# A rebuilt opening of a two-layer diffusion block: tokens first, and shift and scale from float32 products on raw adaLN weights

## The chip, the core and the metric

The kernel runs on one core of one Trainium2 chip. TensorE multiplies (in the rows PE is its products and PEld its weight loads), VectorE (DVE), ScalarE (ACT) and GpSimd (POOL) do the elementwise work, and SyncE (SP) issues the transfers from HBM. The metric is the device time of one execution in microseconds, the median of several runs; less is better.

## The reference

Two layers work on 256 latent tokens and 256 context tokens of width 1024. Ahead of each sublayer every token is normalized, scaled and shifted; shift, scale and gate come from a conditioning vector (`c` for the latent tokens, `c_ctx` for the context tokens) through one wide matrix per layer. Only the first sublayer's start matters here:

```python
def _rms(x, eps=EPS):
    return x * lax.rsqrt(jnp.mean(x * x, axis=-1, keepdims=True) + eps)

def _modulate(x, shift, scale):
    return _rms(x) * (1 + scale) + shift

def _ada_params(cond, w, b):                 # w: (1024, 6144)
    m = jnp.dot(jax.nn.silu(cond), w) + b
    return jnp.split(m[..., None, :], 6, axis=-1)   # sh1, sc1, g1, sh2, sc2, g2

def _chunk_gmlp(h, w_in, norm_g, w_s, b_s, w_out):
    u, v = jnp.split(jax.nn.gelu(h @ w_in), 2, axis=-1)   # v: 2048 columns
    ...

# layer 0, the same for the context tokens with c_ctx
sh1, sc1, g1, sh2, sc2, g2 = _ada_params(c, ada_w[0], ada_b[0])
m_lat = _chunk_gmlp(_modulate(h, sh1, sc1), ...)
```

The rest of layer 0, its FFN, the attention layer and the second FFN are the same before and after the change.

## The kernel before

**Layout.** Activations are kept transposed: `hT[k]` holds channels k\*128 to k\*128+127 (k = 0 to 7) on the partitions and all 512 tokens in the free dimension. A product that needs float32 accuracy is made of three fp32r products: each operand is split into a high part (`xhi`, `whi`, a rounded copy that ACT writes) and a low part (`xlo`, `wlo`, the difference, on DVE), and `mm3` (lines 61 to 63) adds hi·hi, hi·lo and lo·hi.

**Weight stream.** `Stream` (`ws`) brings the weights of all large products in the order of use. `load` issues 512 KB per half of a piece into `raw` (four buffers), `split` makes `whi` and `wlo` from a half, `get` hands a piece to TensorE, and `release` splits the pieces that may come next (two buffers of `whi` and `wlo`).

**The opening** (lines 304 to 467, pool `start`) makes the modulated tokens for the first sublayer and the first quarter of v. It runs over u = 0 to 7; step u makes shift and scale of channel chunk u:

- `a_load(u)`: two transfers of 512 KB, the columns of `ada_w[0]` for scale (w = 1) and shift (w = 0) of chunk u, in `araw`.
- `a_split(u)`: `ahi` by ACT (line 320) and `alo` by POOL for the scale and DVE for the shift (line 322).
- `ada_mm(u)`: sixteen products (lines 327 and 328) whose stationary operand `cvr` has four columns (high and low part of the two conditioning vectors) and whose moving operand is 256 columns of `ahi` or `alo`. The result has 4 partitions; ACT copies it out (`ada_sb`, line 344), two transposes bring it back onto 128 partitions (`ps_adaT`, line 350), and two DVE additions make `mods` (lines 355 and 356).
- `x_modulate(u)`: `modt` (DVE, line 378), `xhi` (ACT, line 382) and `xlo` (DVE, line 384) for both token groups.
- `v_first(u - 2)`: the twelve products of chunk u - 2 with the first 512 columns of v, four token tiles by three parts.

Ahead of that, the four token tiles `xt` (512 KB each) are squared and summed by ACT (line 430), transposed on TensorE (`x_trans`, line 366) and copied to `hT`; `r` is the reciprocal root per token, and `rb` its broadcast through TensorE (`ps_rb`, lines 444 and 448). In the opening the order on ACT, DVE and TensorE is near that of the code (`manual_schedule`); elsewhere a scheduler places the instructions.

**After the opening**, v has three more quarters (96 products each), interleaved with `bg(1)`: background units that accumulate the rest of the adaLN vector on DVE (`ada_acc`, lines 295 and 297) from `ada_raw`, two buffers of 512 KB (line 246), and fold and transpose it in `bg_stage` (lines 256 to 264). Then u, the position mixing (`ps_mix`, line 579) and the rest follow.

Of the kernel before, what the change touches and what calls it, by code (L numbers as in the profile page):

```python
# [11 lines left out]
F32 = mybir.dt.float32  # L12
F32R = mybir.dt.float32r
# [22 lines left out]
def dit_kernel(ctx: ExitStack, tc: tile.TileContext, x, c, cx, c_ctx, ada_w, ada_b, gm_w_in, gm_norm_g,  # L36
# [13 lines left out]
    def f(ap):  # L50
        return ap.bitcast(F32)
# [13 lines left out]
    class Stream:  # L65
# [22 lines left out]
        def split(self, upto, eng=None):  # L88

            while self.ns < min(upto, 2 * len(self.specs)):  # L90
                i, half = self.ns // 2, self.ns % 2
                _, _, kc, _, cols = self.specs[i]
                n = kc * cols
                if half == 0:
                    self.tiles[i] = [wp.tile([P, 2048], F32R, tag=t, name=t, bufs=self.HB)[:, :n] for t in ("whi", "wlo")]
                hi, lo = self.tiles[i]
# [117 lines left out]
        return mods[l][:, which * 8 + kc, cond:cond + 1]  # L214

    cs = cp.tile([P, 2, KC], F32, name="cs")
    cvr = cp.tile([P, KC, 4], F32R, name="cvr")
# [84 lines left out]


    with tc.tile_pool(name="start", bufs=1) as st:
        araw, ahl = {}, {}

        def a_load(u):
            for w in (1, 0):
                t = st.tile([P, KC, P], F32, tag="araw", name="araw", bufs=4)
# [21 lines left out]
        a_load(0)  # L331
        xts = []
        for t in range(4):
            xt = st.tile([P, D], F32, name=f"xt{t}")
            sp.dma_start(xt, (x if t < 2 else cx)[0, (t % 2) * P:(t % 2 + 1) * P, :])
            xts.append(xt)
            if t == 1:
                dma_vecs(1)
        a_load(1)
        ws.load(1)  # L340

        def ada_out(ps, u):
            sb = kp.tile([4, 256], F32, tag="ada_sb", name="ada_sb")
            act.copy(sb, ps[:4, :])
            return sb

        def ada_mods(sb, u):
            pt = aux("ps_adaT")
            for w in range(2):
                pe.transpose(out=pt[:, w * 4:w * 4 + 4], in_=sb[:, w * P:(w + 1) * P], identity=ident[:4, :4])  # L350
            p3 = pt[:, :8].rearrange("p (w c) -> p w c", w=2)
            m = mods[0][:, 0:16, :].rearrange("p (w k) c -> p w k c", w=2)[:, :, u, :]
            ab = adab[:, 0, 0:16].rearrange("p (w k) -> p w k", w=2)[:, :, u:u + 1].broadcast_to([P, 2, 2])
            tmp = kp.tile([P, 2, 2], F32, tag="ada_t", name="ada_t")
            dve.tensor_tensor(tmp, p3[:, :, 0:2], ab, op=ALU.add)
            dve.tensor_tensor(m, tmp, p3[:, :, 2:4], op=ALU.add)

        rb = st.tile([P, T], F32, name="rb")

        xps = {}  # L360

        def x_trans(k, eng):

            ps = acc("ps_xT")
            for t in range(4):
                pe.transpose(out=ps[:, t * P:(t + 1) * P], in_=xts[t][:, k * P:(k + 1) * P], identity=ident)
            xps[k] = ps
            if eng:
                eng(hT[k], ps)

        def x_modulate(k, part=None):

            if part in (None, 0):
                xm[k] = []
                for s in range(2):
                    sl = slice(s * S, (s + 1) * S)
                    t = kp.tile([P, S], F32, tag="modt", name="modt")
                    dve.scalar_tensor_tensor(t, hT[k][:, sl], mod(0, 1, k, s), rb[:, sl], op0=ALU.mult, op1=ALU.mult)
                    xm[k].append((sl, t))
            for s, (sl, t) in enumerate(xm[k]):  # L380
                if part in (None, 1):
                    act.activation(xhi[k][:, sl], t, AF.Identity, bias=mod(0, 0, k, s))
                if part in (None, 2):
                    dve.scalar_tensor_tensor(xlo[k][:, sl], t, mod(0, 0, k, s), f(xhi[k][:, sl]),  # L384
                                             op0=ALU.add, op1=ALU.subtract)

        xm = {}

        def ada_step(u):
            ps = aux("ps_ada", 256)  # L390
            ada_mm(ps, u)
            sb = ada_out(ps, u)
            if u < KC - 1:
                a_split(u + 1)
            if u < KC - 2:
                a_load(u + 2)
            if u < 4:
                ws.split(u + 1)
            if u >= 2:
                v_first(u - 2)  # L400
            ada_mods(sb, u)
            x_modulate(u)

        pss, wv = [], []

        def v_first(k):
# [5 lines left out]
            for t in range(4):  # L412
                mm3(pss[t], xr(k, t * P, (t + 1) * P), (w[0][:, k % 4, :], w[1][:, k % 4, :]),
                    start=k == 0, stop=k == KC - 1)
            if k == 3:
                ws.release()

        with tc.manual_schedule(engines={mybir.EngineType.Activation, mybir.EngineType.DVE, mybir.EngineType.PE}):

            load_vecs(0)  # L420
            act.activation(cs, vecs[:, 0:16].rearrange("p (c k) -> p c k", c=2), AF.Silu)
            act.preload_act_table_set("natural_log_exp_and_others")
            csk = cs.rearrange("p c k -> p k c")
            dve.tensor_copy(cvr[:, :, 0:2], csk)
            dve.tensor_tensor(cvr[:, :, 2:4], csk, f(cvr[:, :, 0:2]), op=ALU.subtract)
            a_split(0)
# [4 lines left out]
            ps_ada = aux("ps_ada", 256)  # L431
            ada_mm(ps_ada, 0)
            load_vecs(1)
            for l in range(2):
                for w in (1, 4):
                    dve.tensor_scalar(adab[:, l, w * 8:w * 8 + 8], adab[:, l, w * 8:w * 8 + 8], 1.0, None, op0=ALU.add)
            x_trans(0, dve.tensor_copy)
            x_trans(1, None)
            x_trans(2, None)
            r = rsqrt(msum, 1.0 / D, 4, "r0")  # L440
            dve.tensor_copy(hT[1], xps[1])
# [4 lines left out]
            sb = ada_out(ps_ada, 0)  # L446
            ada_mods(sb, 0)
            dve.tensor_copy(rb, psr)
            a_split(1, lo=False)
            act.copy(hT[2], xps[2])  # L450
            x_modulate(0, 0)
            a_split(1, hi=False)
            ws.split(1, pool)
            x_modulate(0, 1)
            x_modulate(0, 2)
            for k in range(3, 8):
                x_trans(k, dve.tensor_copy if k in (3, 5, 7) else act.copy)
        a_load(2)
        for u in range(1, KC):
            ada_step(u)  # L460
        for i in range(2, 4):
            dma_vecs(i)
        v_first(KC - 2)
        v_first(KC - 1)
        ws.ahead = True
        ws.release()
        bg_load(2)
# [667 lines left out]
```

## Time and profile before

| what | us |
|---|---|
| median of 3 runs | 1110.42 (1109.51 to 1113.75) |
| the profiled execution | 1113.34 |
| its span on the chip | 1111.6 |
| PE, DVE, ACT, POOL busy in it | 1059.5, 905.6, 547.0, 161.4 |

The span is the stretch from the first to the last instruction; the 1.7 us by which the profiled execution is longer lie around it. Busy time says that an engine had an instruction in work, not that it was at its best. What bounds a stage is read from the stage itself.

### The profile page before, as it was taken

How to read it: one execution, taken by the hardware profiler on the slowest of the kernel's cores; microseconds unless marked ns; L12 is line 12 of the kernel's file. 1: busy time of each engine (PE TensorE's matmuls, PEld its weight loads, DVE VectorE, ACT ScalarE, POOL GpSimd, SP SyncE). 2: the span in 40 equal slices, each digit the busy share in tenths (PEclk: the TensorE clock that was granted, in tenths of full speed). 3: DMA queues.
4: the chain of work that ended last, by engine and by line, in shares of the span. 5: the costliest groups of instructions: out<-in, count | busy, mean ns of one | idle time of the engine just before them, and what ended most of it. 6: DMA issues, size and time to landing. Idle time of an engine off the chain costs nothing.

```text
span 1111.6 us, 15428 instructions
## 1 busy us (share of the span) xinstructions
PE 1059.5 (95%) x5724; PEld 907.3 (82%) x5724; DVE 905.6 (81%) x1518; ACT 547.0 (49%) x921; POOL 161.4 (15%) x131
## 2 busy tenths in 40 slices
PE   4899989999998999999999999989999989999996
PEld 3677868888888888888878888989989878888885
DVE  5978779898999789868686576699988978969696
ACT  6644433323245645224432345456666557757474
POOL 3401101102022011100010002332243040000001
PEclk8999989999999999999999999999999989999998
DMA  8865455544543344676366332333222253565652
GB/s 267 266 210 175 152 171 151 171 138 152 166 146 120 92 147 148 206 225 205 99 205 212 105 118 63 114 106 96 70 84 82 71 171 118 188 200 183 185 176 89
DMA packets 139849, 167.84 MB, mean 151 GB/s; under 512 B 5917, under 2 KB 103934, under 8 KB 139774
## 3 DMA queue, kind: packets, MB, share of 16 engines
q1 hardware_dynamic: 139774, 166.86, 48.1%
q8 instruction: 45, 0.74, 0.3%
q14 instruction: 30, 0.25, 0.1%
HBM read 165.79 MB, written 1.05 MB: 150 GB/s over the span
## 4 chain that ended last, share of the span: by engine, by line
PE 73%; DVE 16%; DMA 4%; issue 3%; ACT 3%; POOL 0%; SPq 0%; DVEq 0%; ACTq 0%; POOLq 0%
PE ps_up L965 7%; PE ps_up L61 6%; PE ps_up L62 6%; PE ps_up L63 6%; PE ps_dn L62 5%; PE ps_dn L63 5%; PE ps_dn L61 5%; DMA ada_raw<-in_ada_w_dram 4%; PE ps_up L967 4%; DVE wlo L101 3%; DVE ada_acc L297 3%; PE ps_u L61 2%; PE ps_u L62 2%; PE ps_u L63 2%; PE ps_wo L62 2%
## 5 line engine op out<-in xcount | busy, mean ns | idle before, releaser
L100 ACT CAST whi<-raw 128x1024 fp32r<-128x1024 f32 (+2 forms) x218 | 218.7, 1023 | 199.9 <-PE ps_dn L62 49.0
L101 DVE TENSOR_TENSOR wlo<-raw,whi 128x1024 fp32r<-128x1024 f32 (+2 forms) x213 | 261.7, 1243 | 51.4 <-ACT whi L100 51.1
L297 DVE SCALAR_TENSOR_TENSOR ada_acc<-ada_raw,cs,ada_acc 128x512 f32<-128x512 f32 x224 | 168.7, 777 | 41.7 <-DMA ada_raw<-in_ada_w_dram 39.7
L63 PE MATMUL ps_up<-xhi,wlo 128*128 128x512 f32 (+1 forms) x384 | 142.4, 372 | 1.0 <-DVE wlo L101 1.0
L61 PE MATMUL ps_up<-xhi,whi 128*128 128x512 f32 (+1 forms) x384 | 143.3, 374 | 0.0
L62 PE MATMUL ps_up<-xlo,whi 128*128 128x512 f32 (+1 forms) x384 | 142.4, 372 | 0.0
L258 POOL TENSOR_TENSOR ada_acc<-ada_acc,ada_half 64x512 f32<-64x512 f32 x16 | 23.4, 1459 | 536.4 <-ACT ada_half L256 397.9
L965 PE MATMUL ps_up<-xhi,whi 128*128 128x512 f32 x352 | 89.7, 397 | 2.5 <-DVE xhi L232 2.5
L63 PEld LDWEIGHTS ps_up<-xhi,wlo 128*128 128x128 f32 x384 | 72.1, 188 | 13.7 <-DVE wlo L101 1.2
L61 PEld LDWEIGHTS ps_up<-xhi,whi 128*128 128x128 f32 x384 | 72.3, 188 | 12.5 <-ACT xhi L231 0.2
L62 PEld LDWEIGHTS ps_up<-xlo,whi 128*128 128x128 f32 x384 | 72.2, 188 | 12.4
L965 PEld LDWEIGHTS ps_up<-xhi,whi 128*128 128x128 f32 x352 | 64.4, 192 | 14.6 <-DVE xhi L232 2.7
L62 PE MATMUL ps_dn<-flo,whi 128*128 128x512 f32 (+1 forms) x200 | 73.0, 365 | 0.7 <-DVE flo L662 0.6
L61 PE MATMUL ps_dn<-fhi,whi 128*128 128x512 f32 (+1 forms) x200 | 73.3, 366 | 0.0
L63 PE MATMUL ps_dn<-fhi,wlo 128*128 128x512 f32 (+1 forms) x200 | 72.7, 364 | 0.0
L61 PE MATMUL ps_wo<-ghi,whi 128*128 128x512 f32 (+1 forms) x160 | 56.1, 354 | 0.1
L62 PE MATMUL ps_wo<-glo,whi 128*128 128x512 f32 (+1 forms) x160 | 55.8, 350 | 0.1
L63 PE MATMUL ps_wo<-ghi,wlo 128*128 128x512 f32 (+1 forms) x160 | 55.7, 349 | 0.0
L61 PE MATMUL ps_u<-xhi,whi 128*128 128x512 f32 x128 | 51.3, 401 | 0.0
L61 PE MATMUL ps_v<-whi,xhi 128*128 128x512 f32 x128 | 51.0, 398 | 0.0
L63 PE MATMUL ps_v<-whi,xlo 128*128 128x512 f32 x128 | 50.2, 393 | 0.6 <-DVE xlo L384 0.6
L967 PEld LDWEIGHTS ps_up<-xhi,wlo 128*128 128x128 f32 x352 | 48.0, 190 | 3.4
(246 smaller groups left out, 2522.5 us busy)
## 6 DMA issues: line engine op xcount, KB each, us to landing
raw<-in_ffn_w_up_dram SPq DMA_DIRECT2D x88, 512.0 KB, 4.2
ada_raw<-in_ada_w_dram SPq DMA_DIRECT2D x80, 512.0 KB, 4.3
raw<-in_ffn_w_down_dram SPq DMA_DIRECT2D x36, 512.0 KB, 3.6
raw<-in_gm_w_in_dram SPq DMA_DIRECT2D x32, 512.0 KB, 4.5
raw<-in_da_w_qkv_dram SPq DMA_DIRECT2D x24, 512.0 KB, 3.7
araw<-in_ada_w_dram SPq DMA_DIRECT2D x16, 512.0 KB, 5.3
raw<-in_gm_w_out_dram SPq DMA_DIRECT2D x16, 512.0 KB, 4.2
raw<-in_ffn_w_down_dram SPq DMA_DIRECT2D x8, 384.0 KB, 3.0
```

Source lines behind the costliest of these rows:

```text
L61: pe.matmul(ps, lhsT=l[0], rhs=r[0], start=start, stop=False)
L62: pe.matmul(ps, lhsT=l[0], rhs=r[1], start=False, stop=False)
L63: pe.matmul(ps, lhsT=l[1], rhs=r[0], start=False, stop=stop)
L100: act.copy(hi[:, sl], raw)
L101: (eng or dve).tensor_tensor(lo[:, sl], raw, f(hi[:, sl]), op=ALU.subtract)
L258: pool.tensor_tensor(a[0][LO, :], a[0][LO, :], t[LO, :], op=ALU.add)
L297: dve.scalar_tensor_tensor(a, raw[:, k, :], cs[:, cd, kc:kc + 1], a, op0=ALU.mult, op1=ALU.add)
L965: pe.matmul(ps, lhsT=wcol(w, k, j)[0], rhs=xhi[k], start=k == 0, stop=False)
L967: pe.matmul(ps[:, :S], lhsT=wcol(w, k, j)[1], rhs=xhi[k][:, :S], start=False, stop=k == KC - 1)
```

## The change: a new order of transfers, and another form of the first products

The token tiles are loaded ahead of the adaLN columns, and `araw` has ten buffers in place of four. `a_split`, `ada_mm`, `ada_out`, `cvr` and the transposes of line 350 go. In their place `ada_mms(u)` multiplies in plain float32: the stationary operand is 128 x 128 of the raw adaLN weights, the moving operand is `csk`, the two conditioning columns. Sixteen products give shift and scale on 128 partitions at once, and `ada_mods` adds the bias in one DVE instruction. `woven(a, b)` emits the products of `b` evenly between those of `a`. POOL has no work in the opening any more. The core of the diff:

```diff
-        def a_split(u, hi=True, lo=True):
-            if hi:
-                ahl[u] = tuple(st.tile([P, KC, 2, P], F32R, tag=t, name=t, bufs=2) for t in ("ahi", "alo"))
-            for w in (1, 0):
-                h, l = (a[:, :, w, :] for a in ahl[u])
-                if hi:
-                    act.copy(h, araw[u, w])
-                if lo:
-                    (pool if w else dve).tensor_tensor(l, araw[u, w], f(h), op=ALU.subtract)
-
-        def ada_mm(ps, u):
-            hi, lo = ahl.pop(u)
-            for kc in range(KC):
-                pe.matmul(ps[:4, :], lhsT=cvr[:, kc, :], rhs=hi[:, kc, :, :], start=kc == 0, stop=False)
-                pe.matmul(ps[:4, :], lhsT=cvr[:, kc, :], rhs=lo[:, kc, :, :], start=False, stop=kc == KC - 1)
+        def ada_mms(u):
+            ps = ada_ps[u] = aux("ps_ada4", 4)
+            def one(w, kc):
+                pe.matmul(ps[:, w * 2:w * 2 + 2], lhsT=araw[u, w][:, kc, :], rhs=csk[:, kc, :],
+                          start=kc == 0, stop=kc == KC - 1)
+            return [lambda w=w, kc=kc: one(w, kc) for w in (1, 0) for kc in range(KC)]
+
+        def ada_mods(u):
+            m = mods[0][:, 0:16, :].rearrange("p (w k) c -> p w k c", w=2)[:, :, u, :]
+            ab = adab[:, 0, 0:16].rearrange("p (w k) -> p w k", w=2)[:, :, u:u + 1].broadcast_to([P, 2, 2])
+            dve.tensor_tensor(m, ada_ps.pop(u).rearrange("p (w c) -> p w c", w=2), ab, op=ALU.add)
+
+        def woven(a, b):
+            n = 0
+            for i, fn in enumerate(a):
+                fn()
+                while n * len(a) < (i + 1) * len(b):
+                    b[n]()
+                    n += 1
...
+            early = [x_trans(k, acc) for k in range(4)]
             for t in range(4):
+                for fns in early:
+                    fns[t]()
                 junk = st.tile([P, D], F32, tag="junk", name="junk")
                 act.activation(junk, xts[t], AF.Square, accum_out=msum[:, t:t + 1])
...
+            woven(ada_mms(0), x_trans(4, acc) + x_trans(5, aux))
+            act.copy(hT[2], xps[2])
+            ada_mods(0)
+            ws.split(1)
+            x_modulate(0)
+            act.copy(hT[3], xps[3])
+            woven(ada_mms(1), x_trans(6, aux) + x_trans(7, acc))
...
+            for u in range(2, KC + 2):
+                if u + 3 < KC:
+                    a_load(u + 3)
+                if u % 2 and u < 8:
+                    ws.load(u // 2 + 2 if u < 7 else 6)
+                if u < KC:
+                    woven(v_mms(u - 2), ada_mms(u))
+                    ada_mods(u)
+                    if u % 2 == 0:
+                        ws.split(u // 2 + 1)
+                    x_modulate(u)
+                else:
+                    woven(v_mms(u - 2), [])
+                if u == 8:
+                    ws.release()
```

TensorE's queue before, where step 2 ends its adaLN products and the products of chunks 0 and 1 with v follow (`ps_ada` is the result on 4 partitions, `ps_v` the v accumulators, the numbers at the names are buffers):

```order
L328 MATMUL ps_ada<-alo,cvr 4x256
L61 MATMUL ps_v<-whi,xhi_96 128x512
L62 MATMUL ps_v<-wlo,xhi_96 128x512
L63 MATMUL ps_v<-whi,xlo_104 128x512
L61 MATMUL ps_v<-whi,xhi_97 128x512
L62 MATMUL ps_v<-wlo,xhi_97 128x512
L63 MATMUL ps_v<-whi,xlo_105 128x512
L61 MATMUL ps_v<-whi,xhi_97 128x512
L62 MATMUL ps_v<-wlo,xhi_97 128x512
L350 MATMUL ps_adaT<-ident,ada_sb 128x4 x2
L327 MATMUL ps_ada<-ahi,cvr 4x256
```

TensorE's queue of the change at the start of step 2, the first products with v:

```order
L388 MATMUL ps_v<-whi,xhi_95 128x512
L320 MATMUL ps_ada_309<-csk,araw 128x2 x2
L388 MATMUL ps_v<-wlo,xhi_95 128x512
L320 MATMUL ps_ada_309<-csk,araw 128x2
L388 MATMUL ps_v<-whi,xlo_103 128x512
L320 MATMUL ps_ada_309<-csk,araw 128x2
L388 MATMUL ps_v<-whi,xhi_95 128x512
```

Sixteen small products with 2 moving columns now stand between the twelve large ones of a step, one or two at a time, where sixteen products of 256 moving columns stood as a block.

The head of SyncE's queue before:

```order
L190 DMA rows_118<-in_c_ctx_dram 8x128
L311 DMA araw<-in_ada_w_dram 128x8x128 x2
L335 DMA xt_125<-in_x_dram 128x1024
L335 DMA xt_127<-in_x_dram 128x1024
L190 DMA rows_129<-in_ada_b_dram 96x128
L335 DMA xt_131<-in_ctx_dram 128x1024
L335 DMA xt_133<-in_ctx_dram 128x1024
L311 DMA araw<-in_ada_w_dram 128x8x128 x2
L83 DMA raw<-in_gm_w_in_dram 128x2x512
L311 DMA araw<-in_ada_w_dram 128x8x128 x3
```

The same place in the change:

```order
L190 DMA rows_117<-in_c_ctx_dram 8x128
L342 DMA xt_120<-in_x_dram 128x1024
L342 DMA xt_122<-in_x_dram 128x1024
L190 DMA rows_124<-in_ada_b_dram 96x128
L342 DMA xt_126<-in_ctx_dram 128x1024
L342 DMA xt_128<-in_ctx_dram 128x1024
L310 DMA araw<-in_ada_w_dram 128x8x128 x4
L83 DMA raw<-in_gm_w_in_dram 128x2x512
L310 DMA araw<-in_ada_w_dram 128x8x128 x4
L83 DMA raw<-in_gm_w_in_dram 128x2x512
L310 DMA araw<-in_ada_w_dram 128x8x128 x6
```

The first adaLN columns move behind the four token tiles, and more of them stand in a row.

## Rows read from the trace of the kernel before

**Rows 1.** Windows: busy us per engine (instructions), TensorE's granted clock, DMA share, GB/s.

```profile
29.00:59.70 30.70, 25.56 (x154) 17.79 (x153) 29.78 (x39) 19.84 (x30) 12.11 (x5) 1.00 0.71 230
59.70:63.10 3.40, 3.40 (x18) 2.14 (x16) 2.99 (x8) 1.05 (x3) 0.00 (x0) 0.50 0.76 228
...
71.50:150.00 78.50, 77.50 (x351) 63.54 (x350) 59.07 (x85) 37.48 (x68) 8.63 (x5) 1.00 0.55 176
```

**Rows 2.** TensorE's waits up to 72 us: total us, times, longest.

```profile
PE ps_ada L328 <- DVE alo L322: 9.0, 4, 5.2
...
PE ps_adaT L350 <- ACT ada_sb L344: 2.5, 2, 1.8
```

**Rows 3.** Timeline of TensorE in the opening: start us, us, instruction.

```profile
54.59 0.40 PE L61 MATMUL ps_v<-whi,xhi 128*128 128x512 f32 x1
54.82 0.40 PE L62 MATMUL ps_v<-wlo,xhi 128*128 128x512 f32 x1
...
71.53 0.39 PE L61 MATMUL ps_v<-whi,xhi 128*128 128x512 f32 x1
```

**Rows 4.** Timeline of ACT in the opening, and the DVE instruction that ends r.

```profile
5.40 1.04 ACT L320 CAST ahi<-araw 128x1024 fp32r<-128x1024 f32 x1 [0.65 <-DMA araw<-in_ada_w_dram]
6.88 1.04 ACT L320 CAST ahi<-araw 128x1024 fp32r<-128x1024 f32 x1 [0.43 <-DMA araw<-in_ada_w_dram]
...
13.16 1.06 ACT L430 ACTIVATE junk<-xt 128x1024 f32<-128x1024 f32 x1
...
15.57 0.16 DVE L163 SCALAR_TENSOR_TENSOR r_wr_r<-r_wr_y,r_wr_r 128x4 f32<-128x4 f32 x1
```

**Rows 5.** Timeline of TensorE from 13 to 18 us.

```profile
13.41 2.42 PE L366 MATMUL ps_xT<-ident,xt 128*128 128x128 f32 x12
15.79 1.16 PE L444 MATMUL ps_rb<-ident,r_wr_r 128*128 128x128 f32 x8
...
17.09 1.09 PE L366 MATMUL ps_xT<-ident,xt 128*128 128x128 f32 x8
```

**Rows 6.** Lines 327, 350 and 444: duration ns min/median/max, first and last start us.

```profile
L327 PEld LDWEIGHTS ps_ada<-ahi,cvr x64: 82/84/125, 8.0 to 62.0; 128*4 128x4 f32 x64
...
L350 PEld LDWEIGHTS ps_adaT<-ident,ada_sb x16: 133/135/138, 16.9 to 65.8; 4*128 4x128 f32 x16
...
L444 PEld LDWEIGHTS ps_rb<-ident,r_wr_r x8: 185/190/190, 15.8 to 16.6; 128*128 128x128 f32 x8
L444 PE MATMUL ps_rb<-ident,r_wr_r x8: 275/275/376, 15.8 to 16.7; 128*128 128x128 f32 x8
```

**Rows 7.** Timeline of TensorE around the transposes of line 350.

```profile
59.25 0.20 PEld L350 LDWEIGHTS ps_adaT<-ident,ada_sb 4*128 4x128 f32 x2 [2.18 <-ACT ada_sb L344]
...
59.46 0.28 PE L327 MATMUL ps_ada<-ahi,cvr 128*4 128x256 f32 x1
```

**Rows 8.** Timeline of TensorE where the granted clock was 0.50.

```profile
27.95 0.63 PE L61 MATMUL ps_v<-whi,xhi 128*128 128x512 f32 x1
...
28.38 0.63 PE L62 MATMUL ps_v<-wlo,xhi 128*128 128x512 f32 x1
```

**Rows 9.** Timeline of DVE and POOL in the opening.

```profile
29.58 2.40 POOL L322 TENSOR_TENSOR alo<-araw,ahi 128x1024 fp32r<-128x1024 f32 x1 [6.01 <-PE ps_adaT L350]
...
29.93 2.33 DVE L378 SCALAR_TENSOR_TENSOR modt<-hT,mods,rb 128x256 f32<-128x256 f32 x1
...
46.65 1.22 DVE L101 TENSOR_TENSOR wlo<-raw,whi 128x1024 fp32r<-128x1024 f32 x1
...
61.00 0.88 DVE L378 SCALAR_TENSOR_TENSOR modt<-hT,mods,rb 128x256 f32<-128x256 f32 x2
...
62.06 0.88 DVE L384 SCALAR_TENSOR_TENSOR xlo<-modt,mods,xhi 128x256 fp32r<-128x256 f32 x2 [0.18 <-ACT xhi L382]
```

**Rows 10.** Timeline after v: DVE's background units, then TensorE's first wait.

```profile
145.50 5.77 DVE L297 SCALAR_TENSOR_TENSOR ada_acc<-ada_raw,cs,ada_acc 128x512 f32<-128x512 f32 x7 [3.60 <-DMA ada_raw<-in_ada_w_dram]
...
155.99 1.11 PE L264 MATMUL ps_adaT<-ident,ada_acc 128*128 128x128 f32 x4 [4.37 <-POOL ada_acc L259]
```

More of the change, by code (lines that the diff above doesn't have):

```diff
@@ L94, in split @@
                 if half == 0:
-                    self.tiles[i] = [wp.tile([P, 2048], F32R, tag=t, name=t, bufs=self.HB)[:, :n] for t in ("whi", "wlo")]
-                hi, lo = self.tiles[i]
+                    self.part = self.tiles[i] = [wp.tile([P, 2048], F32R, tag=t, name=t, bufs=self.HB)[:, :n] for t in ("whi", "wlo")]
+                hi, lo = self.part
                 self.load(self.ns + 1)
@@ L216, in dit_kernel @@
     cs = cp.tile([P, 2, KC], F32, name="cs")
-    cvr = cp.tile([P, KC, 4], F32R, name="cvr")
     hT = [cp.tile([P, T], F32, name=f"hT{k}") for k in range(KC)]
@@ L304, in dit_kernel @@
     with tc.tile_pool(name="start", bufs=1) as st:
-        araw, ahl = {}, {}
+        araw = {}
         def a_load(u):
             for w in (1, 0):
-                t = st.tile([P, KC, P], F32, tag="araw", name="araw", bufs=4)
+                t = st.tile([P, KC, P], F32, tag="araw", name="araw", bufs=10)
                 n0 = w * D + u * P
@@ L312, in a_load @@
                 araw[u, w] = t
[L314 to L328 removed]
+        ada_ps = {}
+        def ada_mms(u):
[15 more added lines that the diff above has]
+                    n += 1
         dma_vecs(0)
[L331 removed]
         xts = []
@@ L338, in dit_kernel @@
                 dma_vecs(1)
+        a_load(0)
         a_load(1)
         ws.load(1)
[L342 to L356, printed above, removed]
@@ L358, in dit_kernel @@
-        rb = st.tile([P, T], F32, name="rb")
[L360 to L365, printed above, removed]
-                pe.transpose(out=ps[:, t * P:(t + 1) * P], in_=xts[t][:, k * P:(k + 1) * P], identity=ident)
[L367 to L402, printed above, removed]
+        a_load(2)
+        a_load(3)
+        ws.load(2)
+        a_load(4)
@@ new lines, in dit_kernel, with x_trans, one, x_modulate @@
+        rb = st.tile([P, T], F32, name="rb")
+        csk = st.tile([P, KC, 2], F32, name="csk")
+        xm, xps = {}, {}
+        def x_trans(k, alloc):
+            ps = xps[k] = alloc("ps_xT")
+            def one(t):
+                pe.transpose(out=ps[:, t * P:(t + 1) * P], in_=xts[t][:, k * P:(k + 1) * P], identity=ident)
+            return [lambda t=t: one(t) for t in range(4)]
+        def x_modulate(k):
+            for s in range(2):
+                sl = slice(s * S, (s + 1) * S)
+                t = kp.tile([P, S], F32, tag="modt", name="modt")
+                dve.scalar_tensor_tensor(t, hT[k][:, sl], mod(0, 1, k, s), rb[:, sl], op0=ALU.mult, op1=ALU.mult)
+                act.activation(xhi[k][:, sl], t, AF.Identity, bias=mod(0, 0, k, s))
+                xm[k, s] = t
+            for s in range(2):
+                sl = slice(s * S, (s + 1) * S)
+                dve.scalar_tensor_tensor(xlo[k][:, sl], xm[k, s], mod(0, 0, k, s), f(xhi[k][:, sl]),
+                                         op0=ALU.add, op1=ALU.subtract)
@@ L404, in dit_kernel, with v_mms @@
         pss, wv = [], []
-        def v_first(k):
+        def v_mms(k):
             if k == 0:
@@ L411, in v_first, with one @@
             w = wv[k // 4]
[L412 to L416, printed above, removed]
+            def one(t, a, b):
+                pe.matmul(pss[t], lhsT=xr(k, t * P, (t + 1) * P)[a], rhs=w[b][:, k % 4, :],
+                          start=k == 0 and a == b, stop=k == KC - 1 and a == 1)
+            return [lambda t=t, a=a, b=b: one(t, a, b) for t in range(4) for a, b in ((0, 0), (0, 1), (1, 0))]
@@ L418, in dit_kernel @@
         with tc.manual_schedule(engines={mybir.EngineType.Activation, mybir.EngineType.DVE, mybir.EngineType.PE}):
             load_vecs(0)
-            act.activation(cs, vecs[:, 0:16].rearrange("p (c k) -> p c k", c=2), AF.Silu)
+            act.activation(csk.rearrange("p k c -> p c k"), vecs[:, 0:16].rearrange("p (c k) -> p c k", c=2), AF.Silu)
             act.preload_act_table_set("natural_log_exp_and_others")
-            csk = cs.rearrange("p c k -> p k c")
-            dve.tensor_copy(cvr[:, :, 0:2], csk)
@@ L425, in dit_kernel @@
-            dve.tensor_tensor(cvr[:, :, 2:4], csk, f(cvr[:, :, 0:2]), op=ALU.subtract)
-            a_split(0)
+            dve.tensor_copy(cs.rearrange("p c k -> p k c"), csk)
             msum = st.tile([P, 4], F32, name="msum")
+            early = [x_trans(k, acc) for k in range(4)]
             for t in range(4):
+                for fns in early:
+                    fns[t]()
                 junk = st.tile([P, D], F32, tag="junk", name="junk")
                 act.activation(junk, xts[t], AF.Square, accum_out=msum[:, t:t + 1])
-            ps_ada = aux("ps_ada", 256)
@@ L432, in dit_kernel @@
[L432 to L439, printed above, removed]
+                if t == 1:
+                    load_vecs(1)
+                    for l in range(2):
+                        for w in (1, 4):
+                            dve.tensor_scalar(adab[:, l, w * 8:w * 8 + 8], adab[:, l, w * 8:w * 8 + 8], 1.0, None,
+                                              op0=ALU.add)
@@ L440, in dit_kernel @@
+            dve.tensor_copy(hT[0], xps[0])
             r = rsqrt(msum, 1.0 / D, 4, "r0")
-            dve.tensor_copy(hT[1], xps[1])
             psr = aux("ps_rb")
@@ L445, in dit_kernel @@
                           start=True, stop=True)
-            sb = ada_out(ps_ada, 0)
-            ada_mods(sb, 0)
+            act.copy(hT[1], xps[1])
             dve.tensor_copy(rb, psr)
-            a_split(1, lo=False)
+            woven(ada_mms(0), x_trans(4, acc) + x_trans(5, aux))
             act.copy(hT[2], xps[2])
[L451 to L460, printed above, removed]
+            ada_mods(0)
[3 more added lines that the diff above has]
+            woven(ada_mms(1), x_trans(6, aux) + x_trans(7, acc))
+            for k in range(4, 6):
+                act.copy(hT[k], xps[k])
+            ada_mods(1)
+            x_modulate(1)
+            for k in range(6, 8):
+                act.copy(hT[k], xps[k])
+            for u in range(2, KC + 2):
[13 more added lines that the diff above has]
+                    ws.release()
         for i in range(2, 4):
             dma_vecs(i)
-        v_first(KC - 2)
-        v_first(KC - 1)
         ws.ahead = True
```

## The prediction, written before the change was run

> **What bounds the opening now.** I read the windows first. From 29.0 to 59.7 us DVE is busy for 29.78 of 30.70 us and TensorE for 25.56, so DVE leads there; from 71.5 to 150 TensorE is busy for 77.50 of 78.50 [rows 1]. The waits say it from the other side: up to 72 us TensorE lost 9.0 us to `alo` and 2.5 to `ada_sb` [rows 2]. DVE is that full for two reasons: it makes the low parts of the adaLN columns, and while POOL makes its share, an instruction of 256 columns on DVE takes 2.33 us where an undisturbed pair takes 0.88 [rows 9]. The first quarter of v ends where its successor starts, at 71.53 us [rows 3]. I call this the **end of the opening**. What follows is TensorE's, so what the change is worth is how far this moment moves, less what a later wait takes back.
>
> **What goes and what it frees.** The high and low parts of 16 tiles leave ACT, DVE and POOL. A step then needs, on DVE, one `mods` addition, two `modt` and two `xlo` (0.88 + 0.88 us) and on average half a `wlo` of 1.22 [rows 9]: about 2.5 us, which the 6 us of TensorE found below cover, as they cover ACT's three instructions. The new wait on DVE is that of `mods` for the step's last small product; behind it stand the `wlo` and `modt` of the same step, which TensorE wants only a step later.
>
> **Transfers.** Now the first `araw` is in work at 5.40 us and the second at 6.88 [rows 4]; the token tiles take these places, so I put them at 5.4, 6.9, 8.3 and 9.7. DMA moved 230 GB/s at a share of 0.71 [rows 1], 324 at a full one, or 1.6 us per 512 KB. On SyncE's queue four adaLN tiles follow (landing at 11.3 to 16.2), the first half of v's weights (17.8), and so on, until the last adaLN tile lands near 41 and v's fourth half near 43. With ten buffers no load waits long for a consumer. Step 7 needs its tiles at about 54 and comes behind them; if loads were slower by a third, they would still be hidden.
>
> **Start.** The last token tile's square starts at 13.16 and `r` is done at 15.73 [rows 4], 2.6 us later. So `r` comes at 12.3, and `ps_rb`, 1.16 us [rows 5], ends at 13.4.
>
> **One small product.** A float32 product shows as two records: the four of line 444 are eight [rows 5, 6]. So a step has 32 small records, each a load of 128 columns and a product of 2. The loads are the cost. A load of 4 columns takes 82 ns, one of 128 columns 190 [rows 6], about 105 more. And line 444's first product, whose load nothing hides, takes 376 ns against 275, 101 more [rows 6]. I take **0.105 us per record**. Lower bound: the two loads of line 350 end within 0.20 us and take 0.135 each [rows 6, 7], so 0.065 apart, but these are of transposes, whose loads are shorter (135 against 190). Upper bound: the first of that pair to the next product is 0.21 us [rows 7], 0.105 per record with a load of 0.065, so 0.04 beyond the load; with a load of 0.105 that makes 0.15. The middle value is nearest to line 444, which is the same kind of product.
>
> The Trainium skill speaks against this form: TensorEngine Tiling (Array Packing), section Performance Considerations, says that a product has some 60 cycles of overhead, so that one moving column costs as much as 60. By it, and 25 ns per record at 2.4 GHz as an estimate, the opening would end 6 us later than I say below, at no gain. The 0.21 us for a pair [rows 7] leaves room for it; the heavy record among the rivals is that case, priced from rows.
>
> **One step.** Products of 512 columns start 0.23 us apart at the full clock [rows 3]. Behind such a product the next load is hidden; of the records woven in (32 on 12, 2.67 each) each then exposes one load, their own or that of the next large one. So 0.23 + 2.67 x 0.105 = 0.51 us per large product and **6.1 us per step**. Steps 0 and 1 are woven into eight transposes, which run some 0.11 us apart (8 in 1.09, with the last one's own time in it) [rows 5]: 8 x (0.11 + 4 x 0.105) = 4.2 us each.
>
> **The sum.** After the wait for `r` the clock may be at half. Before, transposes took 0.20 us each from 13.41 (12 in 2.42), and from 17.09 8 took 1.09 [rows 5]: TensorE had worked on without a pause since 10.1. I let the new one come up at 17. Step 0 starts at 13.4, does 3.4 of its 8 groups at half pace by 17.0, the rest by 19.4; step 1 ends at 23.6. `x_modulate(0)` is ready before (weights at 17.8, then `whi`, `wlo`, `modt`, `xhi` and `xlo`, near 22). Six steps of 6.1 end at 60.2, and the 24 last products, 5.5 us, at **65.7**. That is 5.8 us ahead of 71.5.
>
> **Later.** At 151.6 TensorE waits 4.37 us for a background unit, behind DVE, which had itself waited 3.60 us for `ada_raw` [rows 10]. That chain moves along, since its splits wait for v's pieces to be released. But the third `ada_raw` now goes out behind two more weight halves and `bsb`, and this I price at 0 to 3 us (two or so loads at 1.6), taking 0.6, because these units wait on transfers anyway. Sum: 5.8 - 0.6 = 5.2. The profiled execution took 1113.34, which would be 1108.1; it stands 2.9 above the median, and from the median of 1110.42 I come to **1105.2**.
>
> A change of 0.5%, 5.5 us, is about what a measurement here can tell from none.
>
> **Rivals.**
>
> *Half clock through the weave* (ends on the other side). In the new steps TensorE never rests long, yet more than half of its time goes to loads; no stretch of this trace is like that. The granted clock of 0.50 from 59.7 to 63.1 followed a rest: the load at 59.25 had waited 2.18 us [rows 1, 7]. It came up while products or transposes ran back to back. Whether loads keep it up or bring it up, no row shows. At 0.50, large products start 0.43 us apart [rows 8] and I double the loads: 0.43 + 2.67 x 0.21 = 0.99, 11.9 us per step. Steps 0 and 1 end at 30.2, six steps at 101.6, and the last products, half of them slow, at 109.6: 38 us later than 71.5, **1148**. It decides if the clock is low when step 2 starts and does not rise. Against it: a low clock followed idleness only.
>
> *The clock comes up late*, after one to three steps: 78 to 90 us, so 1117 to 1128.
>
> The Trainium skill has a rule on this: TensorE: Matmul & The Clock Gate, section PE-mode transpose, says that transposes do not count as work for the clock. The transposes from 13.41 on went from 0.20 to 0.14 us while little else ran [rows 5], which speaks against it; by it, steps 0 and 1 would stay at half pace and step 2 start 6 us later, at half clock.
>
> *A light record* of 0.065: 4.8 us per step, step 2 starts at 22.3 (`x_modulate(0)`), the end is at 56.7, **1096**. For it: the pair of line 350. Against it: line 444.
>
> *A heavy record* of 0.15: 7.5 us per step, the end is at 77, 6 us later than before, **1117**. For it: the pair takes longer than its loads. Against it: loads and products of neighbours overlap in all other rows.
>
> *The gain is swallowed* at 151.6, because the chain of background units does not move: **1110**. Against it: those loads follow the splits, which follow TensorE.
>
> **Chances.** The forecast 0.40, with a range of its own of 1100 to 1110, half of it under 1104.9; light record 0.12; half clock 0.28; late clock 0.10; heavy record 0.06; swallowed 0.04. Faster by over 0.5%: 0.20 + 0.12 = 0.32. Within 0.5%: 0.20 + 0.04 and a third of the heavy record, 0.26. Slower: 0.28 + 0.10 + the rest of it, 0.42. The range has to hold both signs: 1096 to 1152 leaves out half of the light records and a little at the top.
>
> **What would show it.** Right: DVE well below full and POOL idle up to 65 us, TensorE waiting only for tokens and `r`; large products about 0.51 us apart in steps 2 to 7; loads of 190 ns; end of the opening near 66; the wait at 151.6 still there, 5 to 6 us earlier. Wrong: a granted clock of 0.50 over steps 2 to 7, large products 1.0 us apart; waits for `araw`; or an earlier end that the background units give back.

## The result and the profile after

The changed kernel takes **1153.62 us** (median of 4 runs, 1152.85 to 1154.53); the kernel before took 1109.97 (4 runs, 1109.08 to 1113.75). The ratio is 1.0378, with a 95% interval of 1.0349 to 1.0406: 3.8% slower. The forecast was 1105.2, and the measured time lies 1.6 us above the top of the range. The profiled execution took 1153.12 us with a span of 1151.3.

What TensorE waits for comes first: waits up to 120 us, with the sum, the number of waits and the longest. They answer to [rows 2].

```profile
PE ps_vec L197 <- DMA rows<-in_c_ctx_dram: 2.7, 1, 2.7
PE ps_xT L362 <- DMA xt<-in_x_dram: 2.7, 2, 2.3
PE ps_rb L416 <- DVE r_wr_r L163: 1.3, 1, 1.3
PE ps_xT L362 <- DMA xt<-in_ctx_dram: 0.8, 2, 0.6
```

The waits for `alo` and `ada_sb` are gone, and after `r` TensorE waits for nothing up to the end of the opening. The windows show the same of the other engines (their columns are busy us with the number of instructions of PE, PEld, DVE, ACT and POOL, then granted clock, DMA share and GB/s); they answer to [rows 1].

```profile
29.50:103.70 74.20, 74.20 (x271) 66.77 (x272) 16.66 (x38) 10.90 (x20) 0.00 (x0) 1.00 0.35 104
```

VectorE, full before, is busy for 16.66 of 74.20 us and POOL not at all. The relief worked, and TensorE, always busy, took 71.7 us (29.47 to 101.15) for the six steps that were to take 36.6. Its timeline says how (start, duration, then the instructions):

```profile
14.54 0.45 PE L362 MATMUL ps_xT<-ident,xt 128*128 128x128 f32 x1
14.78 0.85 PE L320 MATMUL ps_ada<-csk,araw 128*128 128x2 f32 x4
15.50 0.45 PE L362 MATMUL ps_xT<-ident,xt 128*128 128x128 f32 x1
...
29.47 0.77 PE L388 MATMUL ps_v<-whi,xhi 128*128 128x512 f32 x1
...
52.51 0.77 PE L388 MATMUL ps_v<-whi,xlo 128*128 128x512 f32 x1
53.08 0.42 PE L320 MATMUL ps_ada<-csk,araw 128*128 128x2 f32 x2
53.36 0.77 PE L388 MATMUL ps_v<-whi,xhi 128*128 128x512 f32 x1
...
54.64 0.77 PE L388 MATMUL ps_v<-wlo,xhi 128*128 128x512 f32 x1
...
101.15 0.77 PE L388 MATMUL ps_v<-whi,xhi 128*128 128x512 f32 x1
101.72 0.63 PE L388 MATMUL ps_v<-wlo,xhi 128*128 128x512 f32 x1
102.15 0.63 PE L388 MATMUL ps_v<-whi,xlo 128*128 128x512 f32 x1
...
103.77 0.39 PE L388 MATMUL ps_v<-whi,xhi 128*128 128x512 f32 x1
104.00 0.40 PE L388 MATMUL ps_v<-wlo,xhi 128*128 128x512 f32 x1
...
107.88 0.39 PE L61 MATMUL ps_v<-whi,xhi 128*128 128x512 f32 x1
```

Large products start 0.85 us apart (52.51 to 53.36) with two small records between them, and 1.28 us (53.36 to 54.64) with four. When the weave ends at 101.15 they first run 0.43 apart, which is their pace at 1.2 GHz [rows 8], and from 103.77 on 0.23, that of 2.4 GHz [rows 3]. By these durations the clock came up only when products of 512 columns ran alone. The windows view shows 1.00 for 29.5 to 103.7 all the same: durations, not that column, tell the clock here (why is taken up below). The end of the opening moves from 71.53 [rows 3] to 107.88, 36.35 us later. The view of line 320 (minimum, median and maximum of one, in ns) shows the loads:

```profile
L320 PEld LDWEIGHTS ps_ada<-csk,araw x256: 286/333/370, 14.0 to 100.9; 128*128 128x128 f32 x128
```

The same load of 128 columns took 190 ns before [rows 6].

### The profile page after: what moved, and what is told of

It reads as the page before. It is cut to its first block, busy times and chain, and to the rows that moved or that the text cites. A ratio compares the mean times of both kernels' runs of the same rounds, so it can differ in the third digit from the quotient of the medians.

```text
span 1151.3 us, 15559 instructions
## 1 busy us (share of the span) xinstructions
PE 1107.6 (96%) x5836; PEld 957.4 (83%) x5836; DVE 879.3 (76%) x1498; ACT 532.3 (46%) x901; POOL 143.3 (12%) x122
## 4 chain that ended last, share of the span: by engine, by line
PE 77%; DVE 13%; DMA 4%; ACT 3%; issue 2%; POOL 1%; SPq 0%; DVEq 0%; POOLq 0%; ACTq 0%
PE ps_up L950 7%; PE ps_up L61 7%; PE ps_up L62 7%; PE ps_up L63 7%; PE ps_dn L62 5%; PE ps_dn L63 5%; PE ps_dn L61 5%; PE ps_v L388 5%; PE ps_up L952 4%; PE ps_ada L320 3%; DMA ada_raw<-in_ada_w_dram 3%; DVE ada_acc L296 3%; DVE wlo L101 2%; PE ps_u L61 2%; PE ps_u L62 2%
## 5 line engine op out<-in xcount | busy, mean ns | idle before, releaser
L257 POOL TENSOR_TENSOR ada_acc<-ada_acc,ada_half 64x512 f32<-64x512 f32 x16 | 26.3, 1644 | 626.1 <-ACT ada_half L255 454.5
L63 PEld LDWEIGHTS ps_up<-xhi,wlo 128*128 128x128 f32 x384 | 72.2, 188 | 13.7 <-DVE wlo L101 1.2
L320 PEld LDWEIGHTS ps_ada<-csk,araw 128*128 128x128 f32 x256 | 73.4, 335 | 6.9
L320 PE MATMUL ps_ada<-csk,araw 128*128 128x2 f32 x256 | 54.1, 302 | 0.0
```

The source lines that it names most:

```text
L63: pe.matmul(ps, lhsT=l[1], rhs=r[0], start=False, stop=stop)
L257: pool.tensor_tensor(a[0][LO, :], a[0][LO, :], t[LO, :], op=ALU.add)
L320: pe.matmul(ps[:, w * 2:w * 2 + 2], lhsT=araw[u, w][:, kc, :], rhs=csk[:, kc, :], start=kc == 0, stop=kc == KC - 1)
```

## The experiments

The theory after the trace: the weave ran at 1.2 GHz from first to last, because nothing in it brings the clock up (**half clock**). Its rivals: raw float32 products are that dear at any clock (**price**), or the order of the transfers costs it (**order**). Each kernel is compared with the kernel before on its own chip, whose median there was 1112.71 (the first four), 1113.78 (the next four) and 1112.38 (the last). "Opening" is the end of the opening, read as above.

| kernel | time, us | ratio to before, 95% interval | opening | span less opening |
|---|---|---|---|---|
| before (profile) | | | 71.5 | 1040.1 |
| after (profile) | 1153.62 | 1.0378 (1.0349 to 1.0406) | 107.9 | 1043.4 |
| warm | 1124.93 | 1.0100 (1.0083 to 1.0118) | 79.8 | 1044.9 |
| block | 1136.26 | 1.0201 (1.0180 to 1.0222) | 90.7 | 1044.4 |
| swap | 1137.95 | 1.0216 (1.0197 to 1.0234) | 95.0 | 1041.4 |
| tokens | 1118.43 | 1.0041 (1.0027 to 1.0056) | 81.9 | 1034.7 |
| early | 1114.12 | 1.0013 (1.0000 to 1.0026) | 69.6 | 1043.3 |
| tfirst | 1151.47 | 1.0341 (1.0321 to 1.0360) | 104.9 | 1044.7 |
| dose (one run) | 1131.27 | | 87.2 | 1042.3 |
| dveonly | 1105.95 | 0.9933 (0.9914 to 0.9953) | 62.5 | 1040.0 |
| rows | 1113.56 | 1.0013 (0.9998 to 1.0027) | 73.0 | 1040.1 |

**warm: the changed kernel with the clock brought up ahead of step 2.**

```diff
+                if u == 2:
+                    wm = aux("ps_warm")
+                    wt = ws.tiles[0][0].rearrange("p (k n) -> p k n", n=512)
+                    for i in range(16):
+                        pe.matmul(wm, lhsT=xhi[0][:, 0:P], rhs=wt[:, 0, :], start=True, stop=True)
                 if u < KC:
                     woven(v_mms(u - 2), ada_mms(u))
```

> 16 products of 512 columns, whose result nobody reads, stand ahead of the first woven v product; they bring the clock to 2.4 GHz before step 2. Half-clock theory (a small record costs 0.105 us at 2.4 GHz and 0.21 at 1.2; nothing in the weave brings the clock up): the 16 take about 5 us, then slots of 0.51 and steps of 6.1 us, the opening ends near 77 instead of 107.9, and the time is near 1122; if the weave lets the clock fall again, slots return to 1.0 from there on. Price theory (the small records are that dear at any clock): the granted clock shows 1.00, slots stay near 0.9 to 1.0, and the time is 1153.6 + 5 = 1158.

Measured: 1124.93, opening 79.8 where 77 was expected: the 16 products took 6.68 us in place of about 5. The timeline of TensorE:

```profile
29.60 6.68 PE L442 MATMUL ps_warm<-whi,xhi 128*128 128x512 f32 x16 [0.35 <-DVE mods L327]
...
37.16 0.48 PE L388 MATMUL ps_v<-whi,xlo 128*128 128x512 f32 x1
...
38.75 0.48 PE L388 MATMUL ps_v<-whi,xlo 128*128 128x512 f32 x1
```

And its view of line 320:

```profile
L320 PEld LDWEIGHTS ps_ada<-csk,araw x256: 187/192/370, 13.7 to 74.1; 128*128 128x128 f32 x128
```

Three slots take 1.59 us (37.16 to 38.75), 0.53 each instead of 0.995, with the same instructions in them; the loads are back at 192 ns, and the pace lasts to the end of the weave. 16 added products made the kernel 29 us faster than the change was. That rules the price theory out: the same instructions take about half as long once the clock is up. The weave does hold a clock that is up, which the forecast had assumed; it only doesn't raise it.

**tfirst: the sixteen transposes in a row ahead of the small products of steps 0 and 1.**

```diff
-            woven(ada_mms(0), x_trans(4, acc) + x_trans(5, aux))
+            woven(x_trans(4, acc) + x_trans(5, aux), [])
...
+            woven(x_trans(6, aux) + x_trans(7, acc), [])
+            woven(ada_mms(0), [])
...
-            woven(ada_mms(1), x_trans(6, aux) + x_trans(7, acc))
+            woven(ada_mms(1), [])
```

> The changed kernel with the sixteen transposes of steps 0 and 1 in a row ahead of their small products, which then run in two rows of 32 records. Half-clock theory with small products that do not keep the clock: transposes go from 0.25 to 0.14 us apart before 18 us, the first row of small records runs at 0.11, in the second the clock falls, step 2 starts at 1.2 GHz and stays there: 1146 to 1152. If small products keep a clock that is once up: step 2 starts at 24 at 2.4 GHz, 1107 to 1112. By the Trainium skill's rule in TensorE: Matmul & The Clock Gate, section PE-mode transpose, the transposes would stay at 0.25 and nothing changes: 1154.

Measured: 1151.47, as the half-clock theory had it. TensorE's timeline:

```profile
14.73 2.39 PE L362 MATMUL ps_xT<-ident,xt 128*128 128x128 f32 x16
16.96 3.63 PE L320 MATMUL ps_ada<-csk,araw 128*128 128x2 f32 x32
20.84 5.47 PE L320 MATMUL ps_ada<-csk,araw 128*128 128x2 f32 x32 [0.25 <-DVE mods L327]
```

And its windows:

```profile
17.00:24.00 7.00, 6.75 (x56) 6.66 (x55) 2.99 (x6) 2.68 (x5) 0.00 (x0) 0.89 1.16 299
24.00:29.00 5.00, 5.00 (x22) 4.68 (x22) 1.93 (x5) 2.16 (x6) 0.00 (x0) 0.50 1.11 315
29.00:99.00 70.00, 70.00 (x259) 63.18 (x258) 13.73 (x31) 7.64 (x14) 0.00 (x0) 0.50 0.37 113
```

Sixteen transposes start 0.14 us apart on average (14.73 to 16.96); woven, they had stood before their small products by 0.24 (14.54 to 14.78 in the changed kernel). So transposes in a row bring the clock up; the eight `ps_rb` records that run just ahead of them can't have done it alone, since they stand there in the changed kernel too. The first 32 small records then take 3.63 us, 0.112 each; during the second 32, 5.47 us, the clock falls, with one pause of 0.25 us between the two and none behind it (block, below, shows such a fall without any pause). At 24.0 it is 0.50 and stays there for the whole weave, with records of 0.77, 0.85 and 0.42 us as in the changed kernel. So small products in a row do not hold the clock: **a TensorE that does little but load weights loses it, though the engine does not rest.** It also settles the windows view: the same weave at the same pace reads 0.50 here, where the clock had changed before, and 1.00 in the changed kernel, where it had not changed yet since the start of the records.

The Trainium skill, TensorE: Matmul & The Clock Gate, section PE-mode transpose, says that transposes do not count for the clock; 0.14 us against 0.24 shows that here they did. The Trainium skill, TensorE: Matmul & The Clock Gate, section LDWEIGHTS (loading the stationary operand), gives a load as its columns divided by 1.2 in ns, which makes 107 for 128 columns as an estimate; 0.112 us per record is near it at 2.4 GHz, and at 1.2 GHz it is 0.21 (a slot with four records is 1.28 - 0.43 = 0.85 longer than a large product alone), twice that.

**early: steps 0 and 1 with exchanged operands, in rows; the weave as changed.** The 2 columns of condition are loaded and the 128 raw columns move, so that the same products stream columns.

```diff
+        def ada_rows(u):
+            ps = aux("ps_ada", 256)
+            for w in (1, 0):
+                for kc in range(KC):
+                    pe.matmul(ps[:2, w * P:w * P + P], lhsT=csk[:, kc, :], rhs=araw[u, w][:, kc, :],
+                              start=kc == 0, stop=kc == KC - 1)
...
-            woven(ada_mms(0), x_trans(4, acc) + x_trans(5, aux))
+            sb0 = ada_rows(0)
+            woven(x_trans(4, acc) + x_trans(5, aux), [])
...
+            ada_turn(sb0, 0)
```

> Steps 0 and 1 with the operands exchanged (the 2 columns loaded, the 128 raw columns moving), 16 products in a row and the transposes in a row; steps 2 to 7 as in the change. Half-clock theory: the moving columns bring the clock to 2.4 GHz near 17 us, as they did with the operands exchanged everywhere; steps 0 and 1 end at about 25, six woven steps of 6.05 us hold the clock and end at 61.5, the last 24 products at 67, 4 us ahead of the kernel before: 1105 to 1110 beside 1112 (this is the forecast of the prediction, with the clock that it had assumed). Rival: the weave lets the clock fall when nothing but woven products runs: slots return to 1.0, 1150.

Measured: 1114.12, a ratio of 1.0013: as fast as the kernel before, and 37 us better than tfirst on the same chip. The expectation's time was 4 us too low. TensorE's timeline:

```profile
14.36 5.25 PE L329 MATMUL ps_ada<-araw,csk 128*2 128x128 f32 x32
...
20.77 3.65 PE L329 MATMUL ps_ada<-araw,csk 128*2 128x128 f32 x32
...
26.50 0.48 PE L404 MATMUL ps_v<-wlo,xhi 128*128 128x512 f32 x1
...
28.09 0.48 PE L404 MATMUL ps_v<-wlo,xhi 128*128 128x512 f32 x1
```

Moving columns bring the clock up within step 0 (5.25 us for 32 records, then 3.65), the weave starts at 25.80 at 2.4 GHz and holds it: again 1.59 us for three slots (26.50 to 28.09). This kernel comes nearest to what the forecast described, without the 16 products of warm. Its opening ends at 69.6, 1.9 us ahead of before; behind it 3.2 us are lost (1043.3 against 1040.1).

**block: v products in a row, then the small ones, in steps 2 to 7.**

```diff
-                    woven(v_mms(u - 2), ada_mms(u))
+                    woven(v_mms(u - 2), [])
+                    woven(ada_mms(u), [])
```

> The same products unwoven in steps 2 to 7: 12 v products in a row, then the step's 32 small records in a row. Half-clock theory: the v products bring the clock up in the first step or two (24 in a row did so at the end); if it then holds over the small records they take 32 x 0.105 = 3.4 us, a step 6.2, end near 75, time near 1120; if each block of small records lets it fall, they take 32 x 0.21 = 6.8 and a step 10 to 12 us, 1140 to 1154. Price theory: 12 v products at 0.23 and 32 records at 0.21 give 9.6 us per step with a granted clock of 1.00 throughout, about 1139.

Measured: 1136.26, nearest to the price theory's 1139, but by another way, as the timeline shows:

```profile
38.31 0.77 PE L388 MATMUL ps_v<-whi,xhi 128*128 128x512 f32 x1
...
43.58 3.71 PE L320 MATMUL ps_ada<-csk,araw 128*128 128x2 f32 x32
47.15 0.77 PE L388 MATMUL ps_v<-whi,xhi 128*128 128x512 f32 x1
```

The clock swings. Twelve v products run at half pace (38.31 to 43.58, 5.27 us) and bring it up at their end; the 32 small records, which hardly stream a column, enjoy it (3.71 us) and lose it; the next v products start at half pace again. By the price theory the v products would run 0.23 apart.

**swap: exchanged operands in every step, woven.**

```diff
-                pe.matmul(ps[:, w * 2:w * 2 + 2], lhsT=araw[u, w][:, kc, :], rhs=csk[:, kc, :],
+                pe.matmul(ps[:2, w * P:w * P + P], lhsT=csk[:, kc, :], rhs=araw[u, w][:, kc, :],
...
+            for w in range(2):
+                pe.transpose(out=pt[:, w * 2:w * 2 + 2], in_=sb[:, w * P:(w + 1) * P], identity=ident[:2, :2])
...
```

> The small products with their operands exchanged: the 2 columns of condition are loaded, the 128 columns of raw float32 weights move; the result is 2 x 256 and is turned by two small transposes a few products later. Half-clock theory: the same number of records now stream columns instead of loading them, the clock comes up in steps 0 to 2; at about 0.11 us per record a step is 12 x 0.23 + 32 x 0.11 = 6.3 us, the opening ends at 66 to 70, time 1104 to 1113, near or below the kernel before. Price theory (raw float32 products are dear in themselves): slots near 1.0 as now, about 1150. Between: the clock comes up only after some steps, 1115 to 1135.

Measured: 1137.95, a miss for both theories' numbers. The clock did come up in step 0, yet a slot took 0.81 us. The timeline of both TensorE queues around 43 us, and the first product of the step and of the next one, with idle time in brackets:

```profile
41.50 0.49 PE L398 MATMUL ps_v<-whi,xhi 128*128 128x512 f32 x1
...
43.19 0.19 PEld L398 LDWEIGHTS ps_v<-whi,xlo 128*128 128x128 f32 x1 [0.22 <-issue]
43.19 0.50 PE L398 MATMUL ps_v<-whi,xlo 128*128 128x512 f32 x1
43.62 0.09 PEld L320 LDWEIGHTS ps_ada<-araw,csk 128*2 128x2 f32 x2 [0.25 <-issue]
...
51.46 0.49 PE L398 MATMUL ps_v<-whi,xhi 128*128 128x512 f32 x1
```

The load of 2 columns starts 0.43 us after the large product (43.19 to 43.62) where a product's successor comes after 0.23, and the large product's own load starts with it instead of ahead of it. It looks as if a load of another shape than the one before isn't pulled ahead. The weave has 24 such changes per step (not the eight or nine that the next expectation speaks of), and a step takes 9.96 us (41.50 to 51.46). The weave of early has as many alternations, but all its loads have 128 columns, and a slot of it takes 0.53. The next kernel tests it.

**rows: as early, with exchanged operands in rows in every step.**

```diff
-                    woven(v_mms(u - 2), ada_mms(u))
+                    sb = ada_rows(u)
+                    woven(v_mms(u - 2), [], 3, lambda: ada_turn(sb, u))
...
```

> As the kernel with steps 0 and 1 exchanged and in a row, but every step so: 32 small records with exchanged operands in a row, then 12 v products in a row, with the two small transposes after the third. If the exchanged weave was slow because each change between a load of 2 columns and one of 128 leaves the load uncovered (about 0.2 us behind a large product, 0.1 before it), a step has two such pairs instead of eight or nine: 12 x 0.23 + 32 x 0.112 + 0.6 = 7.0 us instead of 9.8, the opening ends near 73 and the time is about 1117. If the exchanged products are slow for another reason, at 0.2 a record, a step stays near 9 us and the time near 1130.

Measured: 1113.56, opening 73.0. The timeline:

```profile
29.57 0.50 PE L406 MATMUL ps_v<-whi,xhi 128*128 128x512 f32 x1
...
32.92 3.65 PE L329 MATMUL ps_ada<-araw,csk 128*2 128x128 f32 x32
36.50 0.50 PE L406 MATMUL ps_v<-whi,xhi 128*128 128x512 f32 x1
```

A step takes 6.93 us (29.57 to 36.50) for the same records that took 9.96 woven; 7.0 was expected. With 4 changes of shape in place of 24 it is 3.0 us shorter, 0.15 a change. That fits the reading that these changes were the cost of swap. The time is 3.4 us below the expectation, since the rest of this kernel took 1040.1 like that of before.

**dose: every second small product of steps 2 to 7 left out.**

```diff
-            return [lambda w=w, kc=kc: one(w, kc) for w in (1, 0) for kc in range(KC)]
+            return [lambda w=w, kc=kc: one(w, kc) for w in (1, 0) for kc in range(0, KC, by)]
...
-                    woven(v_mms(u - 2), ada_mms(u))
+                    woven(v_mms(u - 2), ada_mms(u, 2))
```

> Steps 2 to 7 with every second small product left out (half of the adaLN sum of six column tiles is missing). Half-clock theory, if this thinner weave brings the clock up no more than the full one: slots 0.43 + 1.33 x 0.21 = 0.71, 8.5 us per step, opening ends near 88, 1133. If it brings it up: slots 0.23 + 1.33 x 0.105 = 0.37 after the first step, end near 63, at most 1110. Price theory (0.21 at any clock): slots 0.23 + 1.33 x 0.21 = 0.51, end near 72, 1115, with a clock of 1.00.

Measured: 1131.27 (one run), opening 87.2 where 88 was expected. Three slots with four small records between them lie between these two rows of its timeline:

```profile
39.85 0.77 PE L388 MATMUL ps_v<-whi,xlo 128*128 128x512 f32 x1
...
41.99 0.77 PE L388 MATMUL ps_v<-whi,xlo 128*128 128x512 f32 x1
```

39.85 to 41.99 is 2.14 us, or 0.71 a slot: half clock still. Half as many small products do not let the weave raise the clock either.

**tokens: the kernel before with the token tiles loaded first.**

```diff
         dma_vecs(0)
-        a_load(0)
         xts = []
...
+        a_load(0)
         a_load(1)
         ws.load(1)
```

> The kernel before with one part of the change alone: the token tiles are loaded ahead of the first adaLN tiles. If the order of transfers had a share in the loss, the time is above 1113. By the half-clock theory it has none: r comes 3.4 us earlier, the first adaLN tiles come some 6 us later, and VectorE, which is full, starts its splits later by about that; the time is 1107 to 1116, with a clock as before (1.00 from 29 to 59).

Measured: 1118.43, a ratio of 1.0041: slower, by more than I had expected, so by the expectation's own sign the order of transfers costs something in the kernel before. TensorE's waits up to 165 us begin with these:

```profile
PE ps_ada L327 <- ACT ahi L320: 11.2, 1, 11.2
PE ps_rb L444 <- DVE r_wr_r L163: 6.6, 1, 6.6
PE ps_v L61 <- ACT xhi L382: 3.7, 1, 3.7
```

The first is the later adaLN tile. The second is POOL's doing: three of the four instructions of 128 x 4 that make `r` took VectorE 2.1 to 2.3 us each beside POOL's splits, the last of them 2.26 where it took 0.16 before [rows 4]. The timelines of the two engines, and TensorE's window from 29 to 59 us:

```profile
25.77 2.34 POOL L322 TENSOR_TENSOR alo<-araw,ahi 128x1024 fp32r<-128x1024 f32 x1
25.87 2.26 DVE L163 SCALAR_TENSOR_TENSOR r_wr_r<-r_wr_y,r_wr_r 128x4 f32<-128x4 f32 x1
...
29.00:59.00 30.00, 26.31 (x145) 19.80 (x145) 23.71 (x37) 17.29 (x26) 9.23 (x4) 0.80 0.57 169
```

The granted clock, expected at 1.00 there, was 0.80: it had fallen while TensorE waited. What each of these cost was not tried by itself. The opening ends 10.4 us later (81.9), and 5.4 us come back behind it: no wait for the background unit [rows 10] is left in this trace. The changed kernel has no splits of adaLN tiles, no wait for these tiles, and waits 1.3 us for `r`, so nothing in its trace puts a share of its loss on the order.

**dveonly: the kernel before with another relief for VectorE.** POOL makes no low parts of the adaLN columns, VectorE makes all.

```diff
-                    (pool if w else dve).tensor_tensor(l, araw[u, w], f(h), op=ALU.subtract)
+                    dve.tensor_tensor(l, araw[u, w], f(h), op=ALU.subtract)
```

> The kernel before with another relief for VectorE: it makes the low parts of both adaLN tiles itself and POOL makes none of them. If VectorE's 2.33 us for 256 columns were POOL's doing, a step takes VectorE about 2.5 + 2 x 1.2 = 4.9 us undisturbed instead of 6.1 and TensorE about 5.1: some 5 us gained, 1107. If POOL did not slow it, VectorE has 1.2 us more per step: 6 to 8 us lost, 1119.

Measured: 1105.95, a ratio of 0.9933 (0.9914 to 0.9953), faster than both kernels. VectorE's timeline over one step:

```profile
33.71 0.15 DVE L355 TENSOR_TENSOR ada_t<-ps_adaT,vecs 128x4 f32<-128x4 f32 x1
33.78 1.21 DVE L322 TENSOR_TENSOR alo<-araw,ahi 128x1024 fp32r<-128x1024 f32 x1
...
36.12 0.88 DVE L378 SCALAR_TENSOR_TENSOR modt<-hT,mods,rb 128x256 f32<-128x256 f32 x2
...
38.89 0.15 DVE L355 TENSOR_TENSOR ada_t<-ps_adaT,vecs 128x4 f32<-128x4 f32 x1
```

With twice the splits a step takes it 5.18 us (33.71 to 38.89), and no `modt` takes 2.33 us any more, as one did beside POOL [rows 9]. The view of its line (minimum, median and maximum, in ns):

```profile
L378 DVE SCALAR_TENSOR_TENSOR modt<-hT,mods,rb x16: 475/480/484, 17.4 to 60.0; 128x256 f32<-128x256 f32 x16
```

The opening ends at 62.46, 9.1 us ahead of before. The spans of the two profiled executions differ by the same 9.1 us, the medians on one chip by 7.8.

## Why the prediction was wrong, step by step

- **Start, transfers, VectorE's relief: right.** TensorE waits only for tokens, vectors and `r`; no wait for `araw`; VectorE and POOL as forecast. Step 0 starts 0.8 us late, since `ps_rb` took 2.08 us for its eight records instead of 1.16 [rows 5]: I had given it its price at the full clock, in the same sum that let the clock come up only at 17.
- **One small product: right.** 0.105 us was taken; tfirst and early's weave show 0.112 at 2.4 GHz ((0.53 - 0.23) / 2.67 for the latter), so a slot is 0.53 for 0.51, 1.5 us over 72 slots. At 1.2 GHz 0.21 was taken, and 0.21 measured.
- **The step that failed: "I let the new one come up at 17."** It rested on the transposes of before [rows 5], which ran in a row. Woven among loads of 128 columns they stay 0.96 us apart per group, and the clock does not come up before 103. tfirst shows the two halves apart: transposes in a row raise it, the small products lose it again. That every later step then ran at half pace follows from it: dose, tfirst and the changed kernel show that such a weave does not raise the clock, warm and early that it holds it. Begun at the full clock it took 0.53 us a slot, near the forecast's 0.51; begun at half, 0.995.
- **The reason given against the half-clock rival failed**: "a low clock followed idleness only". In the rows of before the fall had an idle TensorE ahead of it [rows 1, 7], and no stretch had one busy with loads alone, so they could not tell rest from loads. tfirst does: from 17 to 24 us TensorE was busy for 6.75 of 7.00, with loads of 128 columns and 2 columns moving, and the clock fell. The rival, at a chance of 0.28, was the right case.
- **The rival's price was right.** Steps of 11.95 us (11.9 in the prediction), the opening at 107.9 (109.6). "Later" was mis-sized: 0.6 us was taken, and the rest of the changed kernel takes 3.3 us more than that of before (1043.4 against 1040.1), 1.5 of them at the wait for the background unit, now 5.9 us [rows 10]. In the profiled executions 36.35 + 3.3 is the 39.7 us between the spans; the medians differ by 43.65, mostly because the profiled run of before was 3.4 above its median.
- **The forecast, too, would have come out near zero.** early is the nearest to that case: it starts step 2 at 25.8 (23.6 forecast), has slots of 0.53, and loses 3.2 us later. Of the 5.8 us that the opening was to gain, 1.9 are left, and the end gives them back: 1.0013.

What stays open: the rest of these kernels differs from that of before by up to 5 us either way (last column of the table). Each is one execution, and the executions of the kernel before on the last chip lie between 1107.91 and 1115.17 us. Part can be the wait for the background unit, which is 0 to 6.7 us; but in early and warm it is 4.4 us as before, and what makes their rest longer was not tried.

## What to carry to other kernels

When work is moved to TensorE as products with few moving columns, ask what it does to the clock before what it costs: a TensorE that mostly loads weights lost its clock as an idle one does, though the page shows it as busy, and everything woven into it then runs at half pace. Such products go where long products have brought the clock up and still run between them, or they are turned so that the long side moves, in rows of one shape. And an engine that is too full may be relieved by taking its neighbour's work away, where the neighbour holds it up: that one line here was worth more than the rebuilt opening.

## What the runs showed of the hardware

- The granted clock in the windows reads 1.00 before its first recorded change, whatever the pace: 1.00 for slots of 0.85 us in the changed kernel, 0.50 for the same slots in tfirst.
- A weave that cannot raise the clock can hold it: the same instructions ran 72 slots at 0.53 us (early, warm) and at 0.995 (after).
- In swap a load of 2 columns behind one of 128 was not pulled ahead of the running product: 0.43 us from one start to the next where 0.23 is usual; 20 changes of shape less per step made it 3.0 us shorter (9.96 woven, 6.93 in rows).
- POOL's splits hold VectorE up: one `modt` took 2.33 us beside POOL where a pair takes 0.88 [rows 9], and in tokens an instruction of 128 x 4 took 2.26 where it takes 0.16 [rows 4]. With POOL idle (dveonly) none of the sixteen `modt` took over 0.484, so that more work on VectorE took less time.
